# Splitting queries and keys at the projection instead of in the attention

## The chip, the cores and the metric

The kernel runs on one core of a Trainium2 chip. The metric is the device time of one execution in microseconds (us), and a kernel's time is the median of several runs. The core has five engines that run side by side, each with an in-order queue of its own: TensorE (matmuls; PE in the profile, PEld for its weight loads), VectorE (DVE), ScalarE (ACT), GpSimd (POOL) and SyncE (SP), which here does nothing but issue DMAs. TensorE reads its operands from the on-chip memory SBUF and writes its results to PSUM; DMAs move data between SBUF and the chip's main memory (DRAM).

## The reference

One inference step of a one-layer decoder, for a prompt of 2048 new tokens and for 8 sequences of 8 new tokens with 8192 tokens of history each. All arrays are float32. The part that matters here is the prompt's attention with a forgetting term (8 heads of 64 columns):

```python
L = jnp.cumsum(logf, axis=1).transpose(0, 2, 1)
s = jnp.einsum('bqhd,bkhd->bhqk', q_i, k).astype(jnp.float32) * scale      # scale = 64 ** -0.5
s = s + L_i[..., :, None] - L[:, :, None, :]
s = jnp.where(k_pos[None, :] <= q_pos[:, None], s, -jnp.inf)
p = jax.nn.softmax(s, axis=-1)
return jnp.einsum('bhqk,bkhd->bqhd', p.astype(v.dtype), v)
```

`q`, `k`, `v` and the gates come out of one projection `z = x @ w_in`. Beside the attention stands an mLSTM (a matrix memory, 4 heads of 128) over the same tokens, the same two mixers for the 8 sampled sequences (their keys and values are gathered from a paged cache), an output projection with a layer norm, and an MLP of 1024 x 4096 x 1024 with a second layer norm. Keys and values of the prompt are outputs of their own (`k_prompt`, `v_prompt`).

## The kernel before

**Stages.** The projection works through the tokens in four blocks of 512 (the first one with the 64 sampled tokens in front); in each block it makes, one after the other, the mLSTM's values, its queries and keys, the output gate, the attention's queries and keys, and the attention's values. Beside it, `tick` hands out steps of the mLSTM and of the sampled attention. Then come the prompt's attention (`phase_b`), the output projection (`phase_o`) and the MLP (`phase_c`), with the rest of the sampled attention handed out in the last two.

**High and low parts.** A matmul in the fast format fp32r rounds its operands. So a float32 operand x is split: ScalarE writes x rounded to fp32r (`split_hi`, line 154), VectorE writes the remainder x - hi (`split_lo`, line 157), and the products are added up in PSUM. The scores use a special arrangement: the 64 rows of a head's keys stand twice in the 128 partitions, above as hi and below as lo, the queries stand twice as well, and two matmuls (with the queries' hi and lo, lines 1042 and 1043) give all four products.

**The projection's queries and keys (lines 610 to 638).** For each 128 columns (`j` 0 to 3 queries, 4 to 7 keys) and each run of tokens (512 columns in blocks 1 to 3; in block 0 one of 320, of which 64 are sampled, and one of 256), 24 matmuls fill one of four PSUM banks `pm`. ScalarE takes it out in pieces of 256 columns into one of four `st` buffers (line 634), and SyncE stores each piece, queries to a buffer `dq` in DRAM, keys to the output `k_prompt` (line 635). The conv of the mLSTM before it uses two buffers `ac` and two `qi`; the wide loop for the gate and the values behind it uses the same ones as staging.

**The attention.** A unit is a head and 256 queries (`g` 0 to 7); unit g sees 256 (g+1) keys, so units grow within a head. `scores` makes the scores of a unit, and VectorE adds the forget term `nl` and takes the row maximum in one instruction (lines 1050 and 1054; GpSimd prepares the masked diagonal `nd`, line 1035). `values`, one unit behind, exponentiates (ScalarE, line 1071), turns the weights by TensorE (line 1087), copies them out of PSUM (lines 1090 and 1092), multiplies them with the values `vn` (line 1097) and writes a quarter of `ot` (64 x 1024, two buffers; lines 1105 and 1107).

What a unit needs is brought by SyncE's queue, in its order:

- `queries_load` (two units ahead, three `qn` buffers) brings 64 x 256 queries twice; `queries` splits them into `qh` and `ql`, one unit ahead.
- `keys_load` and `keys` do the same for 512 keys at a time into `ks`, of which there are two, for even and odd heads. For the next head this happens during units 0 to 5; for head 0, in its own units.
- `forget_values` brings the head's forget sums `nl` (2048 values, copied to 128 partitions: 1 MB) and its values `vn` (512 KB, rows of 64 columns), for the next head in one go at unit 3.
- At the end of each half of a head (`finish`), three steps are put on the list `ends`, of which each unit takes one at its start: `stores` (the reciprocal sums to DRAM), `sums` (back again, copied to 64 partitions, `rl`) and `scale`, which multiplies `ot` by them on GpSimd (line 1133) and stores it to `dmix` (line 1134). In the very last half VectorE does one of the two multiplications.

**What sets the order.** Each engine's instructions are put into a fixed order when the program is built, by a planner that takes the program's order as priority and its own estimate of when operands are there; an instruction can so stand ahead of its place in the program. On the chip each queue runs strictly in that order. A tile's buffer is free again when the last reader of its earlier content is done; the kernel adds such waits by itself. Pools of one stage lie over those of the stage before, so first uses wait for the old tiles. The first keys and queries of head 0 are loaded by `begin_b` (line 221) before the projection ends, into a pool of their own.

## Time and profile before

| what | value |
|---|---|
| median of 3 runs | 3184.3 us (3182.92 to 3194.81) |
| the profiled execution's own time | 3166.91 us |
| its span, first to last instruction | 3165.1 us |
| TensorE busy | 3076.4 us (97%) |
| VectorE busy | 2125.0 us (67%) |
| ScalarE busy | 1457.3 us (46%) |
| GpSimd busy | 961.5 us (30%) |
| projection | 0 to 860 us |
| prompt's attention | 860 to 1305 us |
| output projection and MLP | 1305 to 3165 us |

Every row of a trace names a line, an engine, an operation and `out<-in`, the tiles that it writes and reads. "x64" is a count, "idle before" is how long the engine stood still ahead of the instruction, and the arrow behind it names what ended that wait. SPq is SyncE's queue: the time of one of its rows is how long issuing took, not the transfer. Matmul ends are modelled, so that a busy TensorE is not one at its peak.

### The profile page before, as it was taken

The numbers are of one execution on the slowest core, as the hardware profiler recorded it, in microseconds if no ns is written. First come the engines' busy times: TensorE is split into PE (matmuls) and PEld (weight loads), VectorE is DVE, ScalarE is ACT, GpSimd is POOL, SyncE is SP. The second block draws the span as 40 slices with busy tenths as digits, with TensorE's granted clock in tenths as the row PEclk, the third lists the DMA queues.
The fourth block names the chain that finished last, engine by engine and source line by source line (L and its number), as shares of the span: only waits on it lengthen the run. The fifth ranks groups of instructions, "written<-read, shape, count | busy, mean of one in ns | idle before, by whom it ended". The sixth has DMA issues, their size and how long they took to land.

```text
span 3165.1 us, 53757 instructions
## 1 busy us (share of the span) xinstructions
PE 3076.4 (97%) x19713; PEld 2425.7 (77%) x19713; DVE 2125.0 (67%) x5095; ACT 1457.3 (46%) x2648; POOL 961.5 (30%) x1046
## 2 busy tenths in 40 slices
PE   8999999999999999899999999999999999999998
PEld 8997787787766676677777777776777776798886
DVE  6857557466487888544566668665676656787888
ACT  4343244334377777422334354443454444455552
POOL 0121232333333334376423334324333222111110
PEclk9999999999999999999999999999999999999999
DMA  5565775777787787487977778978778866587772
GB/s 193 152 212 179 238 234 188 277 267 250 238 269 196 210 211 172 159 303 261 359 277 271 279 274 302 344 263 315 282 280 325 317 226 238 156 266 200 210 203 77
DMA packets 332512, 765.36 MB, mean 242 GB/s; under 512 B 64057, under 2 KB 154681, under 8 KB 331353
## 3 DMA queue, kind: packets, MB, share of 16 engines
q1 hardware_dynamic: 236120, 414.41, 39.9%
q0 software_dynamic: 90864, 330.61, 31.4%
q10 hardware_dynamic: 5264, 16.91, 1.4%
q8 instruction: 156, 2.56, 0.3%
q14 instruction: 108, 0.88, 0.1%
HBM read 709.23 MB, written 93.98 MB: 254 GB/s over the span
## 4 chain that ended last, share of the span: by engine, by line
PE 76%; DMA 11%; issue 5%; DVE 5%; POOL 2%; ACT 1%; SPq 0%; DVEq 0%; POOLq 0%; ACTq 0%
PE py L163 6%; PE py L165 6%; PE ph L163 6%; PE ph L165 6%; PE py L164 6%; PE ph L164 6%; PE pw L1359 5%; PE pm L163 5%; PE pm L165 5%; PE pm L164 5%; DMA y<-cache_v,idxV 3%; PE sO L2245 3%; PE po L1097 3%; DMA vt<-cache_v,idxV 3%; PE sQ L2132 3%
## 5 line engine op out<-in xcount | busy, mean ns | idle before, releaser
L157 DVE TENSOR_TENSOR wl<-wr,wh 128x1024 fp32r<-128x1024 f32 x321 | 393.5, 1230 | 237.3 <-ACT wh L154 235.7
L154 ACT ACTIVATE wh<-wr 128x1024 fp32r<-128x1024 f32 x321 | 337.6, 1055 | 326.0 <-PE ph L164 168.9
L2109 POOL DMA_INDIRECT kT<-cache_k,idxK x256 | 276.5, 1080 | 642.7 <-PE sQ L2132 576.4
L163 PE MATMUL py<-wh,hh 128*128 128x512 f32 x904 | 357.6, 400 | 0.1
L164 PE MATMUL py<-wl,hh 128*128 128x512 f32 x904 | 353.7, 393 | 0.0
L165 PE MATMUL py<-wh,hl 128*128 128x512 f32 x904 | 352.6, 394 | 0.8 <-DVE hl L157 0.8
L1668 DVE TENSOR_TENSOR y<-y,py 128x512 f32<-128x512 f32 x404 | 272.4, 681 | 84.5 <-PE py L165 81.4
L163 PE MATMUL ph<-x1h,wh 128*128 128x512 f32 x768 | 303.8, 396 | 0.0
L2221 POOL DMA_INDIRECT vt<-cache_v,idxV x197 | 203.2, 1032 | 329.8 <-PE sO L2245 257.4
L164 PE MATMUL ph<-x1l,wh 128*128 128x512 f32 x768 | 301.5, 393 | 0.0
L165 PE MATMUL ph<-x1h,wl 128*128 128x512 f32 x768 | 299.9, 393 | 0.0
L163 PE MATMUL pm<-xh,whi 128*128 128x512 f32 (+2 forms) x640 | 231.0, 361 | 0.0
L165 PE MATMUL pm<-xh,wlo 128*128 128x512 f32 (+2 forms) x640 | 228.8, 357 | 0.0
L164 PE MATMUL pm<-xl,whi 128*128 128x512 f32 (+2 forms) x640 | 227.9, 356 | 0.0
L163 PE MATMUL pm<-whi,xh 128*128 128x256 f32 (+4 forms) x624 | 202.1, 325 | 8.0 <-ACT whi L154 8.0
L157 DVE TENSOR_TENSOR wlo<-wra,whi 128x1024 fp32r<-128x1024 f32 (+1 forms) x112 | 141.0, 1261 | 101.1 <-ACT whi L154 100.8
L163 PEld LDWEIGHTS py<-wh,hh 128*128 128x128 f32 x904 | 169.4, 188 | 50.0 <-issue 5.9
L165 PEld LDWEIGHTS py<-wh,hl 128*128 128x128 f32 x904 | 170.1, 188 | 41.5 <-issue 4.9
L164 PE MATMUL pm<-wlo,xh 128*128 128x256 f32 (+4 forms) x624 | 199.5, 320 | 0.6 <-DVE wlo L157 0.6
L165 PE MATMUL pm<-whi,xl 128*128 128x256 f32 (+4 forms) x624 | 199.9, 320 | 0.0
L164 PEld LDWEIGHTS py<-wl,hh 128*128 128x128 f32 x904 | 170.5, 189 | 35.2 <-issue 2.5
L154 ACT ACTIVATE hh<-hq 128x512 fp32r<-128x512 f32 x150 | 94.1, 631 | 215.4 <-PE py L164 150.6
(442 smaller groups left out, 7210.5 us busy)
## 6 DMA issues: line engine op xcount, KB each, us to landing
wr<-w SPq DMA_DIRECT2D x214, 512.0 KB
wra<-w_in SPq DMA_DIRECT2D x104, 512.0 KB
wr<-dw SPq DMA_DIRECT2D x97, 512.0 KB
dw<-w POOLq DMA_DIRECT2D x63, 512.0 KB, 8.6
wr<-w POOLq DMA_DIRECT2D x34, 512.0 KB, 8.4
Rb<-dR SPq DMA_DIRECT2D x128, 128.0 KB
wx<-dw SPq DMA_DIRECT2D x17, 512.0 KB
xn<-xp_t SPq DMA_DIRECT2D x16, 512.0 KB
```

What stands on the lines that cost most here:

```text
L154: last["ACT"] = A.activation(dst, src, AF.Copy, scale=scale)
L157: r = (eng or V).tensor_tensor(dst, src, hi.bitcast(F32), op=OP.subtract)
L163: T.matmul(ps, wh, xh, start=first, stop=False, skip_group_check=shared)
L164: T.matmul(ps, wh, xl, start=False, stop=False, skip_group_check=shared)
L165: last["PE"] = T.matmul(ps, wl, xh, start=False, stop=stop, skip_group_check=shared)
L1097: last["PE"] = T.matmul(po[c:c + 64, q0:], z["vn"][:, k], PTs[k // 4][:, k % 4, q0:], start=(k < 2), stop=(k >= nk - 2), skip_group_check= ...
L1359: last["PE"] = T.matmul(ps, m[t][x][:, k], (wh, wl)[w][hf][k], start=i == 0, stop=i == 23)
L1668: V.tensor_tensor(y, y, ps, op=op)
L2109: G.indirect_dma_start(out=piece(n), out_offset=None, in_=ck, in_offset=IO(ap=idxK[:, b, j // 2, j % 2:j % 2 + 1], axis=0))
L2132: r = T.matmul(pq[h4 * 32:h4 * 32 + 32, hg].rearrange("p (k c) -> p k c", k=2), z["qb"][:, hd], kv, start=(db == 0), stop=(db == 1), skip_ ...
L2221: vx["last"] = G.indirect_dma_start(out=vt.rearrange("p f c -> p (f c)"), out_offset=None, in_=cv, in_offset=IO(ap=idxV[:, b, (kt % 4) * 4 ...
L2245: after_ = T.matmul(po[r:r + 32], z["PT"][:, hg, 2 * f + g, pg].rearrange("p h q -> p (h q)"), vts[f][:, g, hg * 256:(hg + 1) * 256], star ...
```

## The change

Six edits, all in the projection's query and key part and in the attention.

1. The projection writes queries and keys as hi and lo: ScalarE takes the whole 512 (or 256) columns out of PSUM as hi into an `ac` buffer, VectorE computes lo = psum x scale - hi into a `qi` buffer, and two stores of the whole width go to `dq[0]`, `dq[1]` or to the new `dk[0]`, `dk[1]`. The output `k_prompt` is still written, by copies as before.
2. The attention loads these parts and splits nothing: `keys_load` brings hi and lo straight into the two halves of `ks`, `queries_load` both parts, twice, into a tile `q`.
3. Queries are loaded up to four units ahead, into five buffers.
4. `forget_values` for the next head is called four times with a quarter, behind the scores of units 4 to 7, instead of once at unit 3.
5. `scale` runs on VectorE in all halves, and an empty step in `ends` puts it one unit later; `ot` has three buffers.
6. In the mLSTM the exponential of `gsb` moves from ahead of a block's first chunk to behind that chunk's outputs.

```diff
-                for o in range(w % 256, w, 256):
-                    st = pa.tile([128, 256], F32, name="st", bufs=4)
-                    A.activation(st, ps[:, o:o + 256], AF.Copy, scale=scale)
-                    SY.dma_start(O["k_prompt"][jj * 128:(jj + 1) * 128, a:a + 256] if c else dq[jj, :, a:a + 256], st)
+                n = w // 256 * 256
+                hi = pa.tile([128, 512], F32, name="sa", tag="ac", bufs=2)[:, :n].bitcast(F32R)
+                lo = pa.tile([128, 512], F32, name="sq", tag="qi", bufs=2)[:, :n].bitcast(F32R)
+                A.activation(hi, ps[:, w - n:], AF.Copy, scale=scale)
+                V.scalar_tensor_tensor(lo, ps[:, w - n:], scale, hi.bitcast(F32), op0=OP.mult, op1=OP.subtract)
+                for d, x in enumerate((hi, lo)):
+                    SY.dma_start((dk if c else dq)[d, jj * 128:(jj + 1) * 128, a:a + n], x.bitcast(F32))
+                for o in range(w - n, w, 256):
+                    if c:
+                        st = pa.tile([128, 256], F32, name="st", bufs=4)
+                        A.copy(st, ps[:, o:o + 256])
+                        SY.dma_start(O["k_prompt"][jj * 128:(jj + 1) * 128, a:a + 256], st)
                     a += 256
...
-        A.activation(gsb, gsb, AF.Exp)
         for c in range(bi * 4, bi * 4 + 4):
...
+            if c % 4 == 0:
+                A.activation(gsb, gsb, AF.Exp)
...
+        def keys_load(z, g):
+            h = z["h"]
             for d in range(2):
+                SY.dma_start(z["ks"][g][d * 64:d * 64 + 64].bitcast(F32), dk[d, h * 64:h * 64 + 64, g * 512:(g + 1) * 512])
...
         def queries_load(n):
-            h, g = units[n]
-            qn = qns.pop() if qns else pb.tile([128, 256], F32, name="qn", bufs=3)
+            q = qs.pop() if qs else pb.tile([128, 2, 256], F32R, name="q", bufs=5)
             for d in range(2):
-                SY.dma_start(qn[d * 64:d * 64 + 64], dq[h // 2, h % 2 * 64:h % 2 * 64 + 64, g * 256:(g + 1) * 256])
-            return qn
+                SY.dma_start(q[d * 64:d * 64 + 64].bitcast(F32), q_of(*units[n]))
+            return q
...
-                z["ot"] = pb.tile([64, 1024], F32, name="ot", bufs=2)
+                z["ot"] = pb.tile([64, 1024], F32, name="ot", bufs=3)
...
-                    (V if end and q == 0 else G).tensor_tensor(ot[:, s], ot[:, s], rls[q], op=OP.mult)
+                    V.tensor_tensor(ot[:, s], ot[:, s], rls[q], op=OP.mult)
...
-            ends.extend([stores, sums, scale])
+            ends.extend([stores, sums, lambda: None, scale])
...
-                if n + 2 < len(units):
-                    qnext[n + 2] = queries_load(n + 2)
+                while max(qnext) < min(n + 4, 2 * n + 3, len(units) - 1):
+                    m = max(qnext) + 1
+                    qnext[m] = queries_load(m)
...
-                    if g == 3:
-                        forget_values(Z[h + 1], 0, S)
+                if h < 7 and g >= 4:
+                    forget_values(Z[h + 1], g * 512 - 2048, 512)
...
-                if n + 1 < len(units):
-                    queries(Z[units[n + 1][0]], units[n + 1][1], qnext.pop(n + 1))
```

More of the change, by code (lines that the diff above doesn't have):

```diff
@@ L229, in begin_b @@
         for d in range(2):
-            for t, x in (("kn", O["k_prompt"][0:64, 0:512]), ("qn", dq[0, 0:64, 0:256])):
-                r = SY.dma_start(bf[t][d * 64:d * 64 + 64], x)
+            for t, x in (("ks", dk[d, 0:64, 0:512]), ("q", q_of(0, 0))):
+                r = SY.dma_start(bf[t][d * 64:d * 64 + 64].bitcast(F32), x)
                 tc.add_manual_dep(r.ins, at,
@@ L970, in bank, with keys_home, head @@
             return ppb.tile([128, 512], F32, name="pS", bufs=2)
[L972 to L979 removed]
+        def keys_home(h):
+            ks = homes.pop(h, None) or pb.tile([128, 2048], F32R, name=f"ks{h % 2}")
+            return dict(h=h, ks=[ks[:, g * 512:g * 512 + 512] for g in range(4)])
+        def head(z):
+            e = z["h"] % 2
+            z["vn"], z["nl"] = homes.pop("vn", None) or (pb.tile([128, 16, 64], F32, name=f"vn{e}"),
+                                                         pb.tile([128, 2048], F32, name=f"nl{e}"))
+            z["ls"] = pb.tile([128, 32], F32, name="ls", bufs=2)
+            G.memset(z["ls"], 1.0)
         def forget_values(z, a, n):
@@ L1041, in scores @@
                     pS = bank()
-                    T.matmul(pS[:, :w], qh[:, qs], ks[:, a:a + w], start=True, stop=False)
-                    last["PE"] = T.matmul(pS[:, :w], ql[:, qs], ks[:, a:a + w], start=False, stop=True)
+                    T.matmul(pS[:, :w], qh[:, qs], z["ks"][a // 512][:, :w], start=True, stop=False)
+                    last["PE"] = T.matmul(pS[:, :w], ql[:, qs], z["ks"][a // 512][:, :w], start=False, stop=True)
                     tick(0.42)
```

80 lines of the change are left out of this document (25 added, 55 removed).

## The prediction

> **What bounds the kernel now.** I read the busy shares first, then the busy time by stage: time from the span's start, its length, then for PE, PEld, DVE, ACT and POOL the busy time and the number of instructions, the granted clock, the DMA share and GB/s.
>
> ```profile
> span 3165.1 us, 53757 instructions
> PE 3076.4 (97%) x19713; PEld 2425.7 (77%) x19713; DVE 2125.0 (67%) x5095; ACT 1457.3 (46%) x2648; POOL 961.5 (30%) x1046
> ...
> 0.00:860.00 860.00, 839.30 (x5669) 712.86 (x5670) 532.37 (x1543) 317.75 (x647) 225.27 (x255) 0.99 0.66 221
> 860.00:1305.00 445.00, 426.28 (x2938) 298.76 (x2938) 355.94 (x1397) 333.79 (x774) 165.59 (x255) 0.98 0.75 198
> ```
>
> TensorE bounds the whole. The change touches the projection (to 860 us) and the prompt's attention (to 1305). TensorE is idle 20.7 us in the first and 18.7 in the second, where VectorE has 80% and ScalarE 75%. As matmul ends are modelled, a busy PE also hides short waits; so I cut the attention at the ends of its eight heads (the last `ot<-ot,po` addition of each) and compare heads, which all compute the same.
>
> ```profile
> 863.00:938.40 75.40, 66.57 (x429) 44.63 (x427) 61.01 (x254) 53.87 (x127) 26.56 (x44) 0.95 0.79 255
> 938.40:987.10 48.70, 48.59 (x345) 34.62 (x343) 40.66 (x165) 39.02 (x93) 19.84 (x31) 1.00 0.81 246
> 987.10:1043.70 56.60, 53.21 (x362) 37.34 (x361) 44.40 (x173) 40.82 (x97) 22.77 (x33) 0.97 0.91 197
> 1043.70:1100.80 57.10, 53.67 (x362) 37.32 (x361) 45.92 (x173) 41.57 (x97) 20.42 (x33) 0.97 0.75 204
> 1100.80:1153.60 52.80, 52.10 (x362) 36.75 (x361) 44.40 (x173) 40.91 (x97) 22.57 (x36) 1.00 0.82 220
> 1153.60:1206.20 52.60, 51.55 (x363) 36.83 (x362) 44.71 (x173) 40.98 (x97) 21.08 (x31) 1.00 0.85 201
> 1206.20:1257.30 51.10, 50.81 (x359) 36.33 (x357) 39.43 (x161) 38.77 (x93) 21.52 (x31) 1.00 0.78 166
> 1257.30:1305.50 48.20, 47.67 (x338) 33.71 (x337) 34.01 (x128) 36.66 (x77) 9.66 (x15) 1.00 0.27 70
> ```
>
> Three things are to be seen: head 0 takes 75.4 us, heads 2 and 3 some 57, and the last, which prepares no next head, 48.2. Each excess has its own cause, and a fourth sits behind the attention.
>
> **The change part by part.** The sum is made against the profiled execution, 3166.9 us: the span and 1.8 us around it. The median of the three runs, 3184.3, lies 17.4 above; I carry that offset unchanged.
>
> *A, the last scaling on VectorE.* The timeline behind the last head:
>
> ```profile
> 1300.78 14.70 SPq L1345 DMA_DIRECT2D y<-x_prompt  x5
> 1302.41 0.68 DVE L1133 TENSOR_TENSOR ot<-ot,rl 64x512 f32<-64x512 f32 x1 [1.62 <-DMA rl<-drl]
> 1305.61 9.04 POOL L1133 TENSOR_TENSOR ot<-ot,rl 64x512 f32<-64x512 f32 x1 [1.63 <-DVE pad_5x L85]
> 1316.01 2.44 SPq L1247 DMA_DIRECT2D wr<-w_o  x3
> 1329.03 1.06 ACT L154 ACTIVATE woh<-wr 128x1024 fp32r<-128x1024 f32 x1 [20.76 <-DMA wr<-w_o]
> 1330.14 1.22 PE L1359 MATMUL pw<-woh,mh 128*128 128x512 f32 x2 [8.89 <-ACT woh L154]
> ```
>
> Today one half is multiplied by VectorE in 0.68 us and the other by GpSimd in 9.04. SyncE waits for it before it can load a row of x, three `w_o` pieces stand behind, and TensorE ends 8.89 us short of them. With 0.68 in place of 9.04 the loads start 8.4 us sooner. I take -8; bounds 0 (the loads, 12.9 us from issue to use, are slowed by something else) and -8.9.
>
> *B, values in four pieces.* SyncE and what follows it in head 2; head 3 repeats it at 1054.34 with 12.96 us:
>
> ```profile
> 991.87 0.54 SPq L985 DMA_DIRECT2D vn<-v_prompt  x1
> 994.18 16.89 SPq L1134 DMA_DIRECT2D dmix<-ot  x1
> ...
> 1015.65 0.36 ACT L1105 COPY ot<-po 64x256 f32<-64x256 f32 x1 [5.01 <-DMA dmix<-ot]
> 1016.53 0.70 PE L1097 MATMUL po<-PT,vn 128*64 128x256 f32 x2 [2.74 <-DVE ot L1107]
> ...
> 1054.34 12.96 SPq L1134 DMA_DIRECT2D dmix<-ot  x1
> 1016.00:1019.40 3.40, 2.87 (x14) 1.72 (x16) 3.32 (x10) 2.56 (x6) 0.00 (x0) 0.50 0.36 113
> ```
>
> A 512 KB load of values is followed by a store whose issue takes 16.89 us; the output tile (two buffers) waits for that store, ScalarE and VectorE queue behind it, TensorE stops 2.74 us, and for the next 3.4 us it gets half its clock. Quarters make a quarter of that queue (about 4 us), and the third `ot` buffer takes the rest. Heads 2 and 3 then cost what heads 4 and 5 do: 56.6 + 57.1 - 52.8 - 52.6 = -8.3. I take -8; bounds 0 and -8.3.
>
> The Trainium skill (TensorE: Matmul & The Clock Gate, "What's actually happening") lets the half rate set in only after an idle window of about 3.4 us; the 2.74 us here were shorter, so the trace differs, and a short stop costs its length and 1.7 us. By the page, E below stays as it is; by the row, each of its seven waits could bring 1.7 us more, +12.
>
> *C, the splits leave the attention.* Removed, with the two scalings:
>
> ```profile
> L157 DVE TENSOR_TENSOR ql<-qn,qh 128x256 fp32r<-128x256 f32 x64 | 36.6, 579 | 4.1 <-ACT qh L154 3.8
> L154 ACT ACTIVATE qh<-qn 128x256 fp32r<-128x256 f32 x64 | 26.6, 417 | 17.1 <-DMA qn<-dq 7.2 <-PE po L1097 4.9 <-PE pS L1042 3.6
> L157 DVE TENSOR_TENSOR ks<-kn,ks 64x512 fp32r<-64x512 f32 x32 | 23.5, 766 | 0.6
> L154 ACT ACTIVATE ks<-kn 128x512 fp32r<-128x512 f32 x32 | 18.1, 624 | 2.0 <-DMA kn<-k_prompt 2.0
> L1133 POOL TENSOR_TENSOR ot<-ot,rl 64x512 f32<-64x512 f32 x31 | 50.0, 1617 | 128.0 <-DMA rl<-drl 50.0 <-ACT S L1071 36.4 <-ACT PT L1090 28.5
> ```
>
> VectorE loses 36.6 + 23.5 = 60.1 us and gains 31 x 0.684 = 21.2; ScalarE loses 44.7. Most of it lies under TensorE; on the path it is at most the gap from 52.7 to head 7's 48.2, of which a part is only matmuls that moved across my cut (338 against 362). I take a third of it, 1.5 us, in each of heads 1 to 6: -9; bounds 0 and -22 (five heads at -4.4).
>
> *D, head 0.* 75.4 against 52.7 leaves 22.7. The chain of waits inside it (start, length), and the stage's query loads (count, size of one):
>
> ```profile
> 869.09 5.61 DMA qn<-dq
> ...
> 915.61 12.55 DMA nl<-dnl
> 928.18 7.47 DMA qn<-dq
> qn<-dq SPq DMA_DIRECT2D x126, 64.0 KB
> ```
>
> Queries arrive late: their three buffers turn only after a split, and the second load stands behind a 1 MB forget load. Loaded four units ahead into five buffers, split already, with forget and values in quarters, they should not be late after the first units; their bytes double (126 loads of 64 KB become 128 KB, 8 MB more against 88 in the stage, 445 us at 198 GB/s), with some 20 us of lead. Key loads now go straight into the operand buffer that the head before last used, so SyncE waits for its last scores with the query loads queued behind; that lead hides it, and without it a load's 5 us would show. What stays are head 0's own keys and forget sums, still two units ahead. I take half, -11; bounds -2 and -20.
>
> *E, the scaling in VectorE's queue.* This is the added wait. `scale` now stands in an in-order queue with the reductions of the scores behind it; ScalarE's exponentials and then TensorE's transposes wait for those. The waits of today, over the attention:
>
> ```profile
> POOL ot L1133 <- DMA rl<-drl: 50.0, 7, 10.6
> SPq L1134 <- POOL nd L1035: 59.2, 20, 7.7
> ```
>
> GpSimd, which nobody needed, waited seven times, 7.1 us on average and 10.6 at most, for the broadcast sums. The empty step moves `scale` by one unit, 52.7 / 8 = 6.6 us: 0.5 us is left on average and 4 in the worst case. SyncE's 59.2 us of waiting for GpSimd before the stores goes, so the sums also come sooner. I take +4; bounds 0 and +50 (the step buys nothing, and nothing hides it).
>
> *F, the projection.*
>
> ```profile
> L634 ACT ACTIVATE st<-pm x16: 362/383/392, 137.1 to 199.3; 128x256 f32<-128x256 f32 x16
> L561 ACT COPY qi<-pm 128x512 f32<-128x512 f32 x24 | 13.8, 576 | 36.3 <-PE pm L165 32.6 <-DVE qk L575 3.6
> L1668 DVE TENSOR_TENSOR y<-y,py 128x512 f32<-128x512 f32 x404 | 272.4, 681 | 84.5 <-PE py L165 81.4
> dmix<-ot POOLq DMA_DIRECT2D x1, 256.0 KB, 6.4
> 386.36 0.22 ACT L741 ACTIVATE gsb<-gsb 128x16 f32<-128x16 f32 x1 [5.96 <-DMA gsb<-dgs]
> ```
>
> There are 24 pieces of 512 columns and 16 of 256. VectorE gets 24 x 0.68 + 16 x 0.4 = 23 us more on 532; ScalarE 40 new conversions and 32 key copies for its 64 copies: 24 x 0.58 + 48 x 0.38 - 64 x 0.38 = +8 on 318; the stores grow by 12.6 MB on 190 (860 us at 221 GB/s). All of it lies under TensorE's 98%. The thin place is block 0: 16 pieces in 62 us, one every 3.9, through two buffers of each kind where there were four, so a store has 7.8 us less the conversion; a 256 KB store took 6.4. A store that is late holds ScalarE and the weights' split behind it. The `gsb` step behind the first chunk saves part of one 5.96 us wait. I take +3; bounds -1 and +12.
>
> **Sum.** -8 - 8 - 9 - 11 + 4 + 3 = -29: 3166.9 becomes 3137.9, and the median 3184.3 - 29 = 3155.
>
> **The rivals.**
>
> *Hidden anyway.* TensorE's 97% says that splits and bursts cost it little, and DMA is no less busy than before. Then C is 0, B and D are 4 each (other loads take the place of those removed), A stays: -8 - 4 - 4 + 3 + 3 = -10, 3174. Against it: heads differ by up to 9 us with the same work.
>
> *VectorE stuck behind the sums (the other side).* If the engines' order puts `scale` where GpSimd has it today, the seven waits of 7.1 us fall on VectorE. For it: VectorE has 80%, so little room to catch up. Against it: the empty step, and the earlier stores. With E at +50 the sum is -8 - 8 - 9 - 11 + 50 + 3 = +17, 3201; it turns slower once E passes +33, 4.7 us for each of seven waits.
>
> *Quarters that don't relieve the queue.* One value row of a head is 256 bytes in whatever number of loads, and each load carries its own completion; four loads could hold SyncE as long as one. Then B is 0: -21, 3163. The Trainium skill (DMA: Bandwidth & Descriptors, "Measured") asks for batches of 1 MiB and more, and so speaks for this rival; the trace shows the 512 KB load with a 16.89 us issue behind it, which speaks against big loads at this place.
>
> **How the numbers follow.** A measurement of this kernel tells about 0.5% from no change, 16 us here. Forecast 3155, chance 0.56, own range 3138 to 3170; hidden anyway 0.24; quarters without relief 0.10; slower 0.10. Faster: nearly all of the forecast and the quarters, 0.65; same: the hidden case and their edges, 0.25; slower 0.10. The range takes in 3174 and 3163 and leaves out the slower case and the far ends of C and D: 3132 to 3188.
>
> **What would show it.** A: no 9 us multiply behind the attention and a TensorE gap under 2 us before `woh`. B: no store issue over 6 us, heads 2 and 3 within 1 us of 4 and 5. C: VectorE about 39 us busy in head 4, the head near 51. D: head 0 under 66. E: `DVE ot` waiting for `rl` under 10 us in all. F: the projection's end within 4 us of 860. The forecast is wrong if VectorE waits over 30 us for `rl`, or if the heads keep their lengths.

## The result, and the profile after

The changed kernel is slower: 3265.5 us (median of 6 runs, 3257.41 to 3271.69) against 3187.4 us for the kernel before in the same comparison (6 runs, 3182.92 to 3196.14). The ratio is 1.024, 95% interval 1.0217 to 1.0263. I had forecast 3155.

The profiled execution took 3263.1 us, its span is 3261.4. That of before was 3166.9, some 20 us below its own median; so the two traces lie 96 us apart and the medians 78. First the busy shares and the first two stages (start and end, length, busy time and count for PE, PEld, DVE, ACT and POOL, granted clock, DMA share, GB/s):

```profile
span 3261.4 us, 53720 instructions
...
PE 3106.2 (95%) x19713; PEld 2443.3 (75%) x19713; DVE 2104.0 (65%) x5070; ACT 1428.0 (44%) x2560; POOL 916.3 (28%) x1015
...
0.00:871.30 871.30, 845.02 (x5667) 713.55 (x5667) 546.95 (x1578) 326.29 (x656) 229.62 (x255) 0.99 0.70 233
871.30:1395.30 524.00, 445.94 (x2944) 315.89 (x2943) 322.55 (x1337) 298.83 (x679) 123.61 (x226) 0.91 0.70 183
```

The projection went from 860 to 871 us, the attention from 445 to 524. VectorE, ScalarE and GpSimd all have less to do in it than before (322.6 against 355.9 us, 298.8 against 333.8, 123.6 against 165.6), as the change intends. But TensorE now stands still for 78 of the 524 us, where it was 18.7 of 445, and its granted clock fell from 0.98 to 0.91. Behind the attention the trace is 6 us longer than that of before, although 10 us go there (below); from the last value matmul to the end it is 1861 us before, 1868 after and between 1843 and 1862 in the other runs, so I read nothing from these 6 us. The eight heads, cut as before at the last `ot<-ot,po` of each:

```profile
873.40:940.60 67.20, 60.80 (x424) 41.76 (x416) 48.54 (x225) 42.63 (x99) 21.64 (x40) 1.00 0.87 271
940.60:1010.00 69.40, 55.76 (x365) 39.73 (x364) 39.04 (x159) 36.83 (x85) 16.36 (x31) 0.87 0.76 223
1010.00:1080.50 70.50, 56.23 (x362) 40.09 (x362) 39.91 (x165) 36.44 (x84) 17.28 (x29) 0.86 0.76 166
1080.50:1145.80 65.30, 56.19 (x362) 39.52 (x361) 39.93 (x165) 36.68 (x84) 14.94 (x29) 0.92 0.68 186
1145.80:1215.00 69.20, 55.86 (x361) 39.88 (x360) 39.67 (x164) 36.58 (x84) 15.96 (x30) 0.87 0.72 192
1215.00:1283.30 68.30, 56.61 (x362) 39.75 (x361) 39.65 (x165) 36.51 (x84) 16.20 (x29) 0.87 0.74 177
1283.30:1348.10 64.80, 55.58 (x362) 39.36 (x361) 39.61 (x164) 36.42 (x84) 16.62 (x28) 0.90 0.75 163
1348.10:1395.30 47.20, 46.82 (x333) 34.33 (x331) 34.27 (x127) 36.07 (x74) 4.49 (x10) 0.97 0.18 49
```

Head 0 is 8 us shorter than before. Heads 1 to 6, which took 49 to 57, now take 65 to 71. The last one, which loads nothing for a next head, is as it was. The waits of the attention say for what (total, times, longest):

```profile
POOL nd L1029 <- DVE mx L1048: 319.4, 76, 15.3
ACT S L1065 <- DVE mx L1051: 111.3, 33, 11.6
DVE ot L1127 <- DMA rl<-drl: 110.0, 14, 12.0
```

VectorE waits 14 times, 7.9 us on average, for the broadcast sums `rl`; GpSimd and ScalarE then wait for VectorE. One such wait in the timeline, for the second half of head 2 (start, length, and in brackets the idle time before and what ended it):

```profile
1059.21 0.35 DVE L1110 RECIPROCAL lr<-ls 128x32 f32<-128x32 f32 x1
...
1061.10 4.78 SPq L1116 DMA_DIRECT2D drl<-lt  x4
...
1069.96 1.11 SPq L1122 DMA_DIRECT2D rl<-drl  x2
...
1076.86 0.68 DVE L1127 TENSOR_TENSOR ot<-ot,rl 64x512 f32<-64x512 f32 x1 [10.65 <-DMA rl<-drl]
...
1078.23 0.76 PE L1036 MATMUL pS<-ks,q 128*128 128x512 f32 x1 [6.50 <-DVE mx L1048]
...
1078.79 0.94 ACT L1065 ACTIVATE S<-S,mx 128x768 f32<-128x768 f32 x1 [9.98 <-DVE mx L1051]
```

The reciprocal sums are there at 1059.2. They leave at 1061 to 1066, are asked back only at 1070, and have landed at 1077. VectorE stands in front of them for 10.65 us with the scores' reductions queued behind, so TensorE stops for 6.5 us. What follows such a stop, by its clock (last three columns: clock, DMA share, GB/s):

```profile
1071.70:1078.20 6.50, 0.03 (x1) 0.00 (x1) 1.34 (x8) 0.00 (x0) 0.04 (x1) 0.69 0.73 184
1078.20:1081.70 3.50, 3.47 (x15) 2.90 (x16) 2.60 (x11) 1.69 (x5) 0.83 (x2) 0.60 0.53 143
```

There are twelve such stops of 3.9 to 9.4 us, two in each of heads 1 to 6, 70.8 us together. Behind each, TensorE has half its clock for another 2.8 to 6.0 us (5.98 us at 0.50 from 959.0, for instance), 58 us together. The stops and half of these 58 us, some 100 us, are an estimate of what the waits cost. The end of the attention, on the other hand, is as forecast:

```profile
1392.52 0.68 DVE L1127 TENSOR_TENSOR ot<-ot,rl 64x512 f32<-64x512 f32 x1 [2.01 <-DMA rl<-drl]
...
1395.29 0.68 DVE L1127 TENSOR_TENSOR ot<-ot,rl 64x512 f32<-64x512 f32 x1
...
1396.94 1.05 ACT L155 ACTIVATE woh<-wr 128x1024 fp32r<-128x1024 f32 x1
...
1401.63 0.62 PE L1346 MATMUL pw<-woh,mh 128*128 128x512 f32 x2
```

The 9.04 us multiplication is gone, and TensorE no longer waits 8.89 us for `woh`.

### The profile page after: what moved, and what is told of

The parts are those of the page before. It is cut to its first block, busy times and chain, and to the rows that moved or that the text cites. A ratio compares the mean times of both kernels' runs of the same rounds, so it can differ in the third digit from the quotient of the medians.

```text
span 3261.4 us, 53720 instructions
## 1 busy us (share of the span) xinstructions
PE 3106.2 (95%) x19713; PEld 2443.3 (75%) x19713; DVE 2104.0 (65%) x5070; ACT 1428.0 (44%) x2560; POOL 916.3 (28%) x1015
## 4 chain that ended last, share of the span: by engine, by line
PE 72%; DMA 15%; DVE 4%; issue 4%; POOL 2%; ACT 2%; SPq 1%; DVEq 0%; ACTq 0%; POOLq 0%; another core or an unknown queue 0%
PE py L164 6%; PE py L166 6%; PE py L165 6%; PE ph L166 6%; PE ph L164 6%; PE ph L165 6%; PE pm L164 5%; PE pm L166 4%; PE pm L165 4%; PE pw L1346 4%; PE sO L2232 3%; PE sQ L2119 3%; DMA vt<-cache_v,idxV 3%; DMA drl<-lt 3%; DMA rl<-drl 2%
## 5 line engine op out<-in xcount | busy, mean ns | idle before, releaser
L1065 ACT ACTIVATE S<-S,mx 128x1024 f32<-128x1024 f32 (+2 forms) x192 | 171.7, 898 | 111.8 <-DVE mx L1051 111.3
L1036 PE MATMUL pS<-ks,q 128*128 128x512 f32 (+2 forms) x320 | 142.3, 448 | 67.2 <-DVE mx L1048 34.1
```

Source lines behind the costliest of these rows:

```text
L1036: T.matmul(pS[:, :w], qh[:, qs], z["ks"][a // 512][:, :w], start=True, stop=False)
L1065: last["ACT"] = A.activation(sp[:, :w], sp[:, :w], AF.Exp, bias=mx[:, 7:8], accum_out=lp[:, k:k + 1])
```

## The experiments

"Attention" below is the time from the start of the first score matmul to the start of the last value matmul in the profiled execution: 439.3 us before, 518.7 after. A ratio is against the kernel before on the same chip and in the same comparison; its median was 3187 us beside the changed kernel and between 3164 and 3171 beside the others. My theory S at the start was that VectorE is stuck waiting for the sums; its rival Q, that SyncE's earlier and larger query loads are late or hold up the rest. The last column has the waits that the profile puts down to `rl`. GpSimd's idle time directly in front of the scaling is longer, since the profile gives a part of it other names: 126 us before, 194 in e1, 51 in g2, 41 in h2. There is one trace for each run, and traces whose attention has almost the same order differ by 3 to 4 us (e8 and the kernel before, f_proj3 and the changed kernel); smaller differences of the attention say nothing.

| run | ratio, 95% interval | attention | wait for `rl` |
|---|---|---|---|
| changed kernel | 1.024 (1.0217 to 1.0263) | 518.7 | VectorE 110 |
| e1_pool | 1.0098 (1.0078 to 1.0118) | 473.5 | GpSimd 116 |
| e2_vscale (on before) | 1.0201 (1.0178 to 1.0223) | 510.6 | VectorE 89 |
| e3_shallow | 1.0219 (1.0195 to 1.0243) | 508.6 | VectorE 104 |
| e4_pinned | 1.0082 (1.0064 to 1.0099) | 462.7 | VectorE 39 |
| e5_pool_shallow | 1.0093 (1.0065 to 1.0120) | 471.5 | GpSimd 121 |
| e6_pool_onego | 1.0053 (1.0034 to 1.0071) | 467.4 | GpSimd 82 |
| e7_pool_both | 1.0055 (1.0030 to 1.0080) | 463.8 | GpSimd 148 |
| e8_before_end (on before) | 0.9969 (0.9952 to 0.9985) | 435.3 | GpSimd 42 |
| g1_sums | 1.0113 (1.0064 to 1.0162) | 470.8 | VectorE 51 |
| g2_sums_pool | 0.9904 (0.9872 to 0.9937) | 414.5 | GpSimd 30 |
| g3_sums_act | 1.0199 (1.0156 to 1.0242) | 511.4 | VectorE 31 |
| f_proj3 | 1.0247 (1.0202 to 1.0291) | 515.8 | VectorE 111 |
| h1_best | 0.9908 (0.9886 to 0.9930) | 415.0 | GpSimd 27 |
| h2_before_sums (on before) | 0.9934 (0.9912 to 0.9956) | 428.8 | GpSimd 25 |
| h3_g2_onego | 0.9911 (0.9883 to 0.9940) | 410.6 | GpSimd 27 |
| h5_noempty | 1.0048 (1.0027 to 1.0069) | 460.4 | GpSimd 143 |
| h6_half_q | 0.9928 (0.9911 to 0.9945) | 424.3 | GpSimd 101 |
| h7_values_pool | 0.9989 (0.9976 to 1.0003) | 441.8 | GpSimd 116 |

### Is it the scaling on VectorE?

**e1_pool**: the changed kernel, with the scaling back on GpSimd in all halves but the last.

```diff
-                    V.tensor_tensor(ot[:, s], ot[:, s], rls[q], op=OP.mult)
+                    (V if end else G).tensor_tensor(ot[:, s], ot[:, s], rls[q], op=OP.mult)
```

> The changed kernel with the scaling back on GpSimd in all halves but the very last, where both multiplications stay on VectorE. Theory S (VectorE stands still in its queue until the sums are back, 110 us in 14 waits of the changed kernel's profile): those waits leave VectorE, the attention falls from 524 us to 410 to 445, the median to 3165 to 3195. Rival Q (the loads are late: SyncE's query loads wait 87 us for buffers, and everything behind them is late for TensorE whoever scales): the attention stays over 490, the median over 3235.

**e2_vscale**: the kernel before, with the scaling on VectorE in all halves and the empty step. Its two `ot` buffers stay, since a third has no room there.

```diff
-                    (V if end and q == 0 else G).tensor_tensor(ot[:, s], ot[:, s], rls[q], op=OP.mult)
+                    V.tensor_tensor(ot[:, s], ot[:, s], rls[q], op=OP.mult)
-            ends.extend([stores, sums, scale])
+            ends.extend([stores, sums, lambda: None, scale])
```

> The kernel before with one edit: the scaling on VectorE in all halves and the empty step (two ot buffers as before, since a third does not fit there). S: VectorE waits 50 us or more for the sums, the median rises by 25 to 70 us, to 3212 to 3257. Q: the queue is that of before, so the median stays within 12 us of 3187.

**e3_shallow**: the changed kernel with queries two units ahead.

```diff
-                while max(qnext) < min(n + 4, 2 * n + 3, len(units) - 1):
+                while max(qnext) < min(n + 2, len(units) - 1):
```

> The changed kernel with queries loaded two units ahead as before instead of four, five buffers kept. S: VectorE still waits over 70 us for the sums, the median stays at 3230 to 3270. Q: the sums are issued sooner, the waits on VectorE fall under 30 us and the median to 3200 or less.

**e4_pinned**: the changed kernel, where the multiplication may not stand ahead of the last VectorE instruction recorded at its program place.

```diff
+                    with (ExitStack() if end else tc.issue_after(last["DVE"].ins)):
-                    V.tensor_tensor(ot[:, s], ot[:, s], rls[q], op=OP.mult)
+                        V.tensor_tensor(ot[:, s], ot[:, s], rls[q], op=OP.mult)
```

> The changed kernel with the scaling still on VectorE, but held behind the last score reduction of the unit before its place in the program, so that the planner cannot put it earlier. If the planner's early place is what makes VectorE wait (S in its narrow form), the waits fall from 110 us to under 40 and the median to 3185 to 3220. If the sums come later than even that place, or by Q, the waits stay over 70 us and the median over 3235.

Yes, for the larger part. On the kernel before, the scaling on VectorE, with the empty step, makes the attention 71 us longer; this is its row of the waits:

```profile
DVE ot L1133 <- DMA rl<-drl: 89.4, 15, 13.6
```

Taken off VectorE (e1), 45 of the 79 us go; I had expected 410 to 445 us. How far ahead the queries are loaded hardly matters (10 us in the trace, the ratios overlap). Pinning takes 56 us away with the scaling still on VectorE: pinned, the multiplication of the sixth half stands behind 56 diagonal reductions in VectorE's queue, in the changed kernel behind 53. A unit has two of them, so the planner had taken back one and a half units, more than the empty step gives. But e1 left 34 us, and there GpSimd carries the wait. This is its timeline where the sums of head 4's first half are used:

```profile
1158.22 2.47 POOL L1127 TENSOR_TENSOR ot<-ot,rl 64x512 f32<-64x512 f32 x2 [20.67 <-issue]
1160.66 1.69 POOL L1029 TENSOR_TENSOR nd<-nl,dmask 128x128 f32<-128x128 f32 x4
1161.14 0.29 DVE L1048 CUSTOM_DVE_ANT_0 S<-pS,nd 128x128 f32<-128x128 f32 x1 [9.67 <-POOL nd L1029]
...
1161.49 0.80 PE L1036 MATMUL pS<-ks,q 128*128 128x512 f32 x1 [4.73 <-DVE mx L1048]
```

GpSimd stands idle for 20.7 us in front of the multiplication, and the forget diagonals `nd` are queued behind it. The profile names no releaser, but the sums' load was issued only at 1155.0. VectorE waits 9.7 us for the diagonals, then TensorE. My sentence that nobody needed GpSimd was wrong. In front of the first halves' multiplications of heads 2 to 6 it stood for 10 to 18 us before and stands for 11 to 21 in e1; these sums are used 18 to 28 us after they are there before, 28 to 37 in e1 (from the end of the reciprocal to the start of the first multiplication). So the late sums had to be looked at.

### What makes the sums late?

All of these stand on e1_pool. **e5_pool_shallow** adds the edit of e3. **e6_pool_onego** loads the next head's values and forget sums in one go again, and **e7_pool_both** does both:

```diff
                     head(Z[h + 1])
-                if h < 7 and g >= 4:
-                    forget_values(Z[h + 1], g * 512 - 2048, 512)
+                    forget_values(Z[h + 1], 0, S)
```

> The changed kernel with the scaling on GpSimd in all halves but the last, and with the queries loaded two units ahead instead of four (five buffers stay). Its twin with queries four ahead took 1.0098 of the time before, with an attention of 473.5 us against 439.3; TensorE stood still in unit 6 of heads 1, 2, 4, 5 and 6 for some 9 us each and at the start of heads 3 and 7. Theory Q (query loads in front of the sums in SyncE's queue wait for TensorE and hold the sums): the sums come sooner, GpSimd's 117 us of waiting for them fall under 70, attention 450 us or less, ratio 1.003 or less. Theory B (it is the quarters of values and forget sums that fill SyncE's queue in units 5 to 7, so that the stores of the first half's sums go out 27 us after they are there): no more than 6 us better than the twin, the stalls in unit 6 stay.

> The changed kernel with the scaling on GpSimd in all halves but the last, and with the next head's values and forget sums loaded in one go at unit 3 as before, instead of four quarters behind units 4 to 7. Theory B: the stores of the first half's sums are no longer 27 us late, the stalls in unit 6 (some 9 us in each of five heads) go, attention 430 to 450 us, ratio 0.996 to 1.003. Theory Q: the stalls stay, since the four queries ahead still stand before the sums; within 8 us of the twin's 1.0098. A prediction of mine falls if the stores that stand behind the 512 KB of values take 13 to 17 us again and heads 2 and 3 become longer than heads 4 and 5.

> Both of the last two edits together: scaling on GpSimd in all halves but the last, queries two units ahead, values and forget sums in one go. What is left of the change in the attention is that the parts come split from the projection, and a third output buffer. Theory B or Q alone: no better than the one of the two edits that does it, within 5 us. If the two add up, attention 425 to 435 us, 4 to 14 us under the 439.3 of before, which would be what the splits cost on the path; with the projection's +9 and the end's -10 the ratio is then 0.993 to 0.999. If the splits were hidden anyway, attention 439 or more and ratio 0.999 or more.

Neither theory held. The depth is worth 2 us and the quarters 6, and with both undone the attention is still 464: not the 450 or less that the right one should have given alone. **h5_noempty** takes the empty step out of e7 as well, **h6_half_q** in addition loads only the queries' high parts (it leaves the low parts out), and **h7_values_pool** (with all of the queries) moves the value loads to GpSimd's DMA queue.

```diff
-            ends.extend([stores, sums, lambda: None, scale])
+            ends.extend([stores, sums, scale])
...
-                SY.dma_start(q[d * 64:d * 64 + 64].bitcast(F32), q_of(*units[n]))
+                SY.dma_start(q[d * 64:d * 64 + 64, 0].bitcast(F32), q_of(*units[n])[:, 0])
...
-            qh, ql = q[:, 0], q[:, 1]
+            qh, ql = q[:, 0], q[:, 0]
...
-            SY.dma_start(z["vn"][:, a // 128:(a + n) // 128], vp[a:a + n, h * 64:h * 64 + 64].rearrange("(t p) c -> p t c", p=128))
+            G.dma_start(z["vn"][:, a // 128:(a + n) // 128], vp[a:a + n, h * 64:h * 64 + 64].rearrange("(t p) c -> p t c", p=128))
```

> The version with the scaling on GpSimd, queries two ahead and values in one go (sums in SyncE's queue; attention 463.8 us), without the empty step. If it is the empty step that puts the multiplication where the next forget diagonals wait behind it: attention 445 us or less. If it is the sums' later return (doubled query loads in front of them in SyncE's queue): attention 458 to 475, since the step changes nothing of when they come.

> The version with the scaling on GpSimd, queries two ahead, values in one go and no empty step (attention 460.4 us), which loads only the high part of the queries, 128 KB a unit as the kernel before; the scores' second matmul takes the high part again. It leaves the low parts of the queries out and does the same number of matmuls. If the doubled query loads hold the sums back: the first halves' sums go out under 10 us after they are there, attention 445 us or less. If not: attention 455 or more.

> The same version with all of the queries, whose value loads (512 KB in rows of 256 bytes) go through GpSimd's DMA queue, the sums still through SyncE's. If the values fill SyncE's queue in front of the sums: no issue in SyncE's queue longer than 5 us, the sums go out under 10 us after they are there, attention 415 to 435 us. If the queue is slow for all that it carries, or GpSimd's own work suffers from issuing the values: attention 450 or more.

The empty step makes no difference either (460.4 against 463.8). SyncE's queue in h5, where the sums were there at 1108.3:

```profile
1112.70 0.55 SPq L1000 DMA_DIRECT2D vn<-v_prompt  x1
1113.35 22.17 SPq L1011 DMA_DIRECT2D q<-dq  x2
1135.62 0.54 SPq L1128 DMA_DIRECT2D dmix<-ot  x1
1136.27 0.57 SPq L1011 DMA_DIRECT2D q<-dq  x1
1137.28 1.30 SPq L1116 DMA_DIRECT2D drl<-lt  x4
```

Behind a 512 KB value load SyncE stands for 22 us in two query loads, and the sums go out 29 us late. At the same place in the kernel before, the four small stores got out ahead of the stop (`drl<-lt` at 1109.8, the next load at 1125.5). In its heads 2 and 3 they did not: there they went out 20 us late, and GpSimd waited 18.2 and 16.6 us. Both suspects, the query loads and the value loads, have a share. With half the query loads the attention falls by 36 us, although three issues of 13 to 19 us remain; the sums of only two of the five later first halves go out under 10 us after they are there. With the values out of SyncE's queue no single issue in the attention is over 4 us, and the attention falls by 19 us, not to the 415 to 435 expected. h6 also moves 8 MB less, so it does not tell the room in the queue from the load on the DMA engines; that stays open.

### The sums out of SyncE's queue

**g1_sums** moves the sums' stores and loads in the changed kernel to GpSimd's DMA queue; **g2_sums_pool** is e1_pool with the same; **g3_sums_act** is g1 with ScalarE's queue (`A` for `G`).

```diff
-                    SY.dma_start(drl[h, o:o + 1024].rearrange("(t a q) -> a t q", a=4, q=32)[a], lt[a * 32 + half * 8:a * 32 + half * 8 + 8])
+                    G.dma_start(drl[h, o:o + 1024].rearrange("(t a q) -> a t q", a=4, q=32)[a], lt[a * 32 + half * 8:a * 32 + half * 8 + 8])
...
-                    SY.dma_start(rls[q], dap(drl, h * S + o + q * 512, [[0, 64], [1, 512]]))
+                    G.dma_start(rls[q], dap(drl, h * S + o + q * 512, [[0, 64], [1, 512]]))
```

> The changed kernel with one thing moved: the small stores of a half's sums and the loads that bring them back go through GpSimd's DMA queue instead of SyncE's. Scaling stays on VectorE. Theory S2 (the sums are late because they stand in SyncE's queue behind the loads of values, forget sums and queries, and VectorE is stuck behind them): the sums come back some 6 to 8 us after they are there instead of 17 to 25, VectorE's 110 us of waiting fall under 30, the attention goes from 518.7 us to 440 to 460, ratio 0.998 to 1.006. Rival (the planner puts the scaling so early that any round trip through the chip's memory is too long): waits stay above 60 us, attention above 480, ratio above 1.01.

> As the run before (the sums go through GpSimd's queue), and the scaling also on GpSimd in all halves but the last, so that neither SyncE's queue nor VectorE is touched by the sums. Its twin with the sums in SyncE's queue had an attention of 473.5 us and 1.0098. If the sums' place in SyncE's queue is what kept the rest, the stalls of 9 us in unit 6 go and the attention is 425 to 440 us, ratio 0.993 to 0.999. If it is the work on GpSimd itself (the forget diagonals behind the multiplication), the attention stays above 460.

> The changed kernel with the sums' stores and loads in ScalarE's DMA queue, scaling on VectorE. Theory S2 again: the sums come sooner, VectorE waits less than 40 us for them; but ScalarE then waits for each store to land before it issues the load, some 2 us in each of 15 halves, and its exponentials behind it: attention 450 to 480 us, ratio 1.000 to 1.010. If queue place doesn't matter: attention above 500.

g2 takes the whole loss away. Its heads 1, 3 and 5, and GpSimd's waits for the sums' stores (before it issues the loads) and for the sums:

```profile
938.30:988.90 50.60, 50.60 (x362) 36.96 (x361) 37.25 (x160) 37.18 (x85) 29.76 (x52) 1.00 0.91 287
...
1039.50:1090.20 50.70, 50.70 (x363) 37.06 (x362) 37.28 (x161) 37.30 (x85) 23.88 (x42) 1.00 0.91 254
...
1140.80:1191.40 50.60, 50.60 (x362) 36.96 (x361) 37.24 (x160) 37.08 (x85) 25.43 (x42) 1.00 0.97 241
```

```profile
POOL rl L1122 <- DMA drl<-lt: 46.1, 12, 6.0
...
POOL ot L1127 <- DMA rl<-drl: 29.5, 8, 4.7
```

All six middle heads take 50.6 us with TensorE busy throughout at full clock. The attention is 25 us shorter than before and the kernel 0.9904, the lowest here, with h1 and h3 inside its interval. The two edits work together: the sums' queue alone (g1) brings 48 us, the engine alone (e1) 45, both 104.

But these runs change more than the queue, since the planner orders the instructions anew for each edit. In g1 the sums do not come sooner throughout: in the first halves of heads 2 to 6 they are used 16 to 21 us after they are there (17 to 25 in the changed kernel), in the second halves of heads 1 to 6 16 to 21 (15 to 17). VectorE's waits in these second halves still fall from 8 to 11 us to 3 to 6, because the multiplication stands two or three diagonal reductions later in its queue, behind 55 in the sixth half. A part of the 48 us is thus the later place, as in e4. VectorE waits 14 times, 3.7 us on average; neither the return in 6 to 8 us nor the waits under 30 us in all that I expected came. From e1 to g2 the first halves' multiplications keep their place among the diagonals, and there the sums come sooner (22 to 26 us instead of 28 to 37); in the second halves they again stand two or three diagonals later. No run moves the queue and keeps the places, so how much belongs to which stays open.

g3 cuts VectorE's wait to 31 us and gains 7, where I expected 450 to 480 for the attention. In its trace ScalarE waits 85 us at instructions whose wait is put down to DMAs, 17.3 of them to the sums' stores; in the changed kernel it has no such wait. So ScalarE is held in VectorE's place; by which step of the DMAs is not shown.

### The terms of the sum

**e8_before_end**: the kernel before, with both multiplications of the very last half on VectorE.

```diff
-                    (V if end and q == 0 else G).tensor_tensor(ot[:, s], ot[:, s], rls[q], op=OP.mult)
+                    (V if end else G).tensor_tensor(ot[:, s], ot[:, s], rls[q], op=OP.mult)
```

> The kernel before with one word changed: in the very last half both multiplications by the sums stand on VectorE, not one of two. My term A: the 9.04 us multiplication on GpSimd goes, the TensorE gap before the output projection falls from 8.9 us to under 2, 8 to 10 us in all, ratio 0.9968 to 0.9975. The rival (the loads behind it are late anyway): ratio 0.999 or more.

It gives 0.9969 (0.9952 to 0.9985), so 10 us of 3168.7, and in its trace the stretch from the attention's end to the hundredth `pw` matmul is 10.2 us shorter. Term A is shown.

**f_proj3**: the changed kernel, with block 0's high parts in `st` buffers and its low parts in all four wide ones.

```diff
-                hi = pa.tile([128, 512], F32, name="sa", tag="ac", bufs=2)[:, :n].bitcast(F32R)
-                lo = pa.tile([128, 512], F32, name="sq", tag="qi", bufs=2)[:, :n].bitcast(F32R)
+                if n == 256:
+                    hi = pa.tile([128, 256], F32, name="st", bufs=4).bitcast(F32R)
+                    lo = (pa.tile([128, 512], F32, name="sa", tag="ac", bufs=2) if (a - t0) // 256 % 2 else
+                          pa.tile([128, 512], F32, name="sq", tag="qi", bufs=2))[:, :n].bitcast(F32R)
```

> The changed kernel, where in block 0 of the projection the high parts go to the four 256 column buffers that the key copies use, and the low parts take all four wide buffers in turn, instead of two and two. My term F (the stores of block 0's parts don't get out of two buffers in time): the 8 us that block 0's query and key loop became longer fall to 4 or less, the projection ends 4 to 8 us sooner, and the whole is 3 to 10 us under the changed kernel's 1.024. Rival (the extra conversions, or the bandwidth of the stores, whatever their buffers): block 0 stays within 2 us of the changed kernel.

In the trace block 0's query and key loop ends 2.1 us later than before instead of 8.0, and the projection 3.8 us later instead of 10.4. The timed ratio, 1.0247 (1.0202 to 1.0291), cannot show a gain of that size. What block 0 waited for in the changed kernel stands in the waits of 135 to 212 us:

```profile
ACT sa L639 <- DVE qr L631: 17.2, 3, 6.2
...
DVE sq L640 <- DMA dq<-sq: 7.8, 3, 3.4
...
ACT sa L639 <- DMA dq<-sa: 5.0, 1, 5.0
ACT sa L639 <- DMA dk<-sa: 3.3, 1, 3.3
```

The last three rows are stores that hold a buffer. The first and longest ends with VectorE's copy of the sampled queries (`qr`), which stands in the same queue as the conversions `sq` that wait for stores; whether it is late for that is not shown.

**h1_best** is g2 with the edit of f_proj3. **h2_before_sums** is the kernel before with e8's edit and the sums in GpSimd's queue. **h3_g2_onego** is g2 with values and forget sums in one go (the edit of e6).

> The changed kernel with the scaling on GpSimd in all halves but the last, the sums through GpSimd's DMA queue, and block 0's parts in more buffers. Without the last of these it was 0.9904 of before, with a projection 7.6 us longer. If the buffers work here as they did alone, the projection ends 3 to 7 us sooner, ratio 0.988 to 0.9895; if a shorter projection only moves the wait into the attention's first loads, 0.990 to 0.992.

> The kernel before with its sums in GpSimd's DMA queue and both last multiplications on VectorE; splits, queries, values and output buffers as before. It tells what of the 25 us that the changed kernel's attention gained is owed to the sums' place alone. If the sums' place is all: attention 415 to 422 us. My terms B, C and D: heads 2 and 3 keep their stop behind the values (about 56 us each), head 0 stays above 70 us, heads 4 to 6 are within 1 us of 52, attention 433 to 440, ratio 0.996 to 0.999.

> The version with the sums in GpSimd's queue and the scaling on GpSimd (attention 414.5 us, heads 1 to 6 at 50.6 each), with values and forget sums of the next head in one go at unit 3 instead of in quarters. My term B (one load of values holds SyncE's queue 13 to 17 us, and a store, an output buffer and TensorE with it): some heads become 2 to 5 us longer, attention 417 to 424. If the third output buffer alone takes that stop: attention within 1 us of 414.5.

h1's projection ends 2.0 us sooner than g2's, and the ratio is the same within the intervals. In h2 the attention is 10.5 us shorter than in the kernel before and 6.5 shorter than in e8, which differs from h2 in the sums' queue alone. Heads 2 and 3, which I had expected to stay at 56, fall from 56.6 and 57.1 (56.5 and 53.7 in e8) to 52.8 and 52.9, although values still come in one load and there are two `ot` buffers. No single issue behind a value load takes over 6.1 us there, so the long store and the late sums went together and cannot be told apart. In h3 the loads in one go cost nothing: heads 1 to 6 again take 50.6 us each, with this in SyncE's queue:

```profile
982.50 0.38 SPq L1000 DMA_DIRECT2D vn<-v_prompt  x1
983.42 23.78 SPq L1011 DMA_DIRECT2D q<-dq  x2
```

A queue that stands for 24 us did no harm where nothing short of time stood in it.

## Why the prediction was wrong

The step that failed is E, "I take +4". It rested on three claims.

The first is the size of the wait, seven times 7.1 us and 10.6 at most. That is the one row which names `rl`. GpSimd's multiplication of before stood still seven times more, under other names:

```profile
POOL ot L1133 <- ACT S L1071: 36.4, 3, 18.2
...
POOL ot L1133 <- ACT PT L1090: 28.5, 2, 15.4
...
POOL ot L1133 <- issue: 6.8, 1, 6.8
...
POOL ot L1133 <- DMA qn<-dq: 4.5, 1, 4.5
```

The multiplication reads only `ot` and `rl`, and these seven waits end 2.8 to 4.8 us after the sums' load was issued, as the named ones do (2.8 to 7.6). So there were 14 waits, 126 us in all and 18.2 at most, and VectorE took over 14 waits of 110 us. With 126 in place of 50 the prediction's own sum for the slower side is -8 - 8 - 9 - 11 + 126 + 3 = +93; the traces lie 96 apart, the medians 78. That it comes so near is partly luck, since B, F and the half clocks came out otherwise.

The second claim, that the empty step moves the scaling by 6.6 us, is wrong: the planner put it ahead of its place, behind 53 diagonal reductions where the pinned one (e4) stands behind 56. The third, that "the sums also come sooner", did not come true: they are used 15 to 17 us after they are there in the second halves of heads 1 to 6 (12 to 16 before) and 17 to 25 in the first halves of heads 2 to 6 (18 to 28 before). SyncE's 59.2 us of waiting for GpSimd went, but 87.3 us of waiting for a free query buffer came (21 times, for TensorE).

The rival *VectorE stuck behind the sums* had the mechanism, and "VectorE waits over 30 us for `rl`" was the right sign to look for; its price was not 50 us but about 104 (518.7 against g2's 414.5), which the 100 us of stops and half clock nearly make up. Of that, 45 to 56 us go with the engine (e1 from the changed kernel, g2 from g1) and 48 to 59 with the queue and the order that comes with it (g1 from the changed kernel, g2 from e1). The doubled query bytes of D are not needed for the loss: e2 loses 71 us without them. They matter where GpSimd scales (h6 is 36 us under h5, with 8 MB less moved). There the "some 20 us of lead" covered the queries, but not the sums that stand in the same queue.

The rest, by the prediction's own signs:

- **A** (-8): right, -10 in e8 and in the trace of the changed kernel.
- **B** (-8): store issues stayed under 6 us as said (the longest issue of the attention is 4.0 us for one DMA), but heads 2 and 3 did not come to 4 and 5. The stop existed, and its cure is not the quarters: h2 removes it without them, and h3 shows them worth nothing. The rival *quarters that don't relieve the queue* is right in its effect; by e1 the queue still stood up to 9.5 us in single quarters. And head 3 did not repeat head 2: TensorE's stop there, 2.41 us, ends at 1055.67, when the store's long issue (from 1054.34) had only begun; before it GpSimd had waited 10.56 us for sums, until 1049.74.
- **C** (-9): right in size. From h2 to g2 heads 1 to 6 fall from 311.4 to 303.8 us together and the last from 47.5 to 46.4, so -9, with splits gone and VectorE at 37 us a head (the third output buffer and the deeper queries are in that difference too). In the changed kernel VectorE was busy 39.7 us in head 4, as forecast (39), and the head took 69.
- **D** (-11): head 0 took 67.2 against 75.4, where I had asked for under 66; in h3 it is 63.8. The term is -8 to -12.
- **F** (+3): mis-sized. The projection ended 10.4 us later, within my bound of +12 but not within 4 us of 860. The place was right (block 0, two buffers of each kind); that it is stores which don't get out is shown for some of the waits only. f_proj3 takes 6 of the 8 us there.
- ***Hidden anyway*** fell: without the waits the attention is 25 to 29 us under that of before (g2, h3), against the -28 that I had put on B, C and D together. That the sizes agree is partly luck, since the kernel before gets 6.5 to 10.5 us of it from the sums' queue alone (h2 against e8 and against before). (The rival's sum counts E with +3 instead of +4; with +4 it is -9, 3175.)
- The stops were each followed by a piece at half clock, as the prediction's row had it (0.60 over the 3.5 us behind the 6.5 us stop shown, of which a part is back at full clock). At the 1.7 us worked out there, twelve of them would cost 20 us; the 58 us at half clock cost some 29, an estimate. My +4 had no part of it.

## What to carry to other kernels

Before you move an operation to another engine, list what is queued behind it on the new engine and price the latest, not the usual, arrival of its operands. Add up all the waits of the instruction that moves, not only the row that names the operand. A wait that nobody noticed on one engine can stop the bound of the whole kernel on another. A step in the program is not a delay where a planner may hoist the instruction: only a dependence is. And a short round trip through memory is better kept out of the queue of the big loads: with GpSimd scaling and those loads doubled, the trip of the first halves took up to 37 us instead of 28, and moving it to another queue, with the new order that came with it, was worth 59 us, more than the 29 that the change had aimed at.

## What was not expected of the hardware

- GpSimd's 64x512 multiplication takes 1.26 to 1.30 us in g2 (30 of them). In the kernel before its median is 1.28 as well, but three take 1.84 to 1.88 and the one in the last half 9.04. What slowed the last one was not tried.
- TensorE had about half its clock behind a stop as short as 2.57 us in the projection (0.59 over the 3.5 us from 155.4, in the changed kernel).
- A 512 KB value load is followed by issues of 13 to 24 us in SyncE's queue in the kernel before (in heads 2 and 3), and in several heads of e6, h3, h5 and h6; in h2 by none over 6.1 us. In h3 no head is longer for it.
- Moving small DMAs to another queue came with 48 and 59 us (the changed kernel to g1, e1 to g2), with the same bytes moved but the instructions in another order. The Trainium skill (DMA: Bandwidth & Descriptors, "Issuing engines are not separate DMA queues") says that spreading DMAs over issuing engines saves only the sequencer's time to start them, which is usually small beside the DMA itself. In the row of h5 above SyncE takes 22.17 us to start two query loads, with the sums queued behind; so the measurement decides here, and that time was not small.
